# Eight short reads between the sixth and the seventh load of a row-maximum kernel

## The chip, the cores and the metric

The kernel runs on one core of a Trainium2 chip. The metric is device time in microseconds; a time is the median of its runs. A span is that of one profiled execution, between the first and the last instruction that the profiler saw, and is somewhat shorter than the time.

## The reference

```python
def setup_inputs():
    batch, seq, dim = 32, 512, 1024
    return {"x": np.random.randn(batch, seq, dim).astype(np.float32)}

def reference(x):
    return np.max(x, axis=-1).astype(np.float32)
```

The input is 32 x 512 = 16384 rows of 1024 float32, 67.11 MB. Each row gives one number, its maximum; the output is 65.5 KB. Every input element is read once and takes part in one comparison.

## The kernel before

The 16384 rows are seen as 128 partitions with 128 row indices each. A load brings n row indices of all partitions, so 128 x n rows or n x 512 KB, into a ring of 47 places in on-chip memory. The loads' sizes are in BLOCKS: 18 large ones, and then four pieces (PIECES) that bring the last two row indices in parts.

```python
BLOCKS = [
    [2, 15, 16, 14, 11, 11, 10, 10, 8, 8, 7],
    [3, 3, 3, 2, 1, 1, 1],
]
RING = 47
PIECES = [(532, 492), (592, 432)]
```

All loads are issued by SyncE (SP in the profile), one after the other. A load is issued in the program's order as soon as its places in the ring have been read by the work that stands before it:

```python
    def issue():
        nonlocal issued
        while issued < len(loads):
            start, n, src, _ = loads[issued]
            if any(readers[j] and s < start + n and start < s + k
                   for j, (s, k, _, _) in enumerate(loads[:issued])):
                return
            load = nc.sync.dma_start(out=rows(issued), in_=src)
            issued += 1
        ...
        while pieces:
            nc.sync.dma_start(out=pieces[0][0], in_=pieces[0][1])
            pieces.pop(0)
```

VectorE (DVE) does most of the maxima, a load at a time, with one instruction along the last axis:

```python
    def maximum(out, in_):
        return in_turn("DVE", nc.vector.reduce_max(out=out, in_=in_, axis=X))
    ...
    def direct(j):
        _, n, _, col = loads[j]
        m = shared[j][0]
        k = 0 if lead[j] else m
        maximum(res[:, col + k:col + k + n - m], rows(j)[:, k:k + n - m, :])
```

A part of the last loads is shared with the other engines: TensorE (PE) transposes it, ScalarE (ACT) copies it out of PSUM, GpSimd (POOL) reduces over the partitions, and TensorE brings the result back (`turn` and `back` in the whole kernel). The order in which all of it is written down is PLAN: d is a whole reduction on VectorE, t and b the way over the other engines, p, m and f the rest.

The waits are not written in the kernel. The language's scheduling layer works them out and gives every DMA a completion semaphore. It has eight of them for DMAs and hands them out in turn, in the program's order, numbered 0 to 7: the first load has number 0, the eighth number 7, the ninth number 0 again. A DMA that is given a semaphore whose last user may still be under way is made to wait for that user's completion.

Of the kernel before, what the change touches and what calls it, by code (L numbers as in the profile page):

```python
# [8 lines left out]
F32 = mybir.dt.float32  # L9
# [31 lines left out]
def kernel(  # L41
# [5 lines left out]
    nc = tc.nc  # L47
# [10 lines left out]
    once = ctx.enter_context(tc.tile_pool(name="once", bufs=1))  # L58
# [12 lines left out]
    def in_turn(engine, inst):  # L71
        if engine in latest:
            tc.add_manual_dep(inst.ins, latest[engine].ins.name, NOSYNC, reason="in turn")
        latest[engine] = inst
        return inst

    def maximum(out, in_):
        return in_turn("DVE", nc.vector.reduce_max(out=out, in_=in_, axis=X))  # L78

    ident = once.tile([P, P], F32)  # L80
    colno = once.tile([P, P], F32)
    rowno = once.tile([P, 32], F32)
# [3 lines left out]
        out=colno, data0=ident, data1=ident, initial=-1.0, op0=ALU.add, op1=ALU.mult))  # L86
    in_turn("DVE", nc.vector.transpose(out=rowno, in_=colno[:, :32]))  # L87
    for q in range(1, P // 32):
        part = rowno[q * 32:(q + 1) * 32, 0:1]
        in_turn("DVE", nc.vector.tensor_scalar(  # L90
            out=part, in0=part, scalar1=float(q * 32), scalar2=None, op0=ALU.add))
    identity = in_turn("DVE", nc.vector.tensor_scalar(  # L92
        out=ident, in0=colno, scalar1=rowno[:, 0:1], scalar2=None, op0=ALU.is_equal))
# [41 lines left out]
    def rows(j):  # L135
        start, n, _, _ = loads[j]
        return ring[:, I + start * D:I + (start + n) * D].rearrange("p (i d) -> p i d", d=D)
# [90 lines left out]
    issued = 0  # L228
    behind = None
# [7 lines that stand above are left out]
                return  # L237
            load = nc.sync.dma_start(out=rows(issued), in_=src)  # L238
            issued += 1
        if any(readers[j] and s < at + last + 1 and at < s + k for j, (s, k, _, _) in enumerate(loads)):  # L240
            return
        while pieces:
            nc.sync.dma_start(out=pieces[0][0], in_=pieces[0][1])
            pieces.pop(0)

    for step in PLAN:
        issue()
        kind, k = step[0], int(step[1:])
        if kind in "dp":
            (direct if kind == "d" else partial)(k)  # L250
            readers[k] -= 1
        elif kind == "t":
            turn(k)
            readers[chunks[k][0]] -= 1
        elif kind == "b":
            back(k)
        elif kind == "m":
            merge(k)
        else:
            inst = maximum(*tail[k])  # L260
            if behind is None:
                behind = inst
# [34 lines left out]
```

## Time and profile before

| | before |
|---|---|
| time, median of 3 runs | 163.78 us (163.76 to 163.86) |
| span of the profiled execution | 162.1 us |
| busy: DVE | 135.3 us (83%) |
| busy: POOL | 15.9 us (10%) |
| busy: PE | 13.6 us (8%) |
| busy: ACT | 6.3 us (4%) |
| read from HBM | 67.11 MB, 414 GB/s over the span |

The profile's page gives busy time by engine, the same in 40 equal slices (each digit is the busy share of a slice in tenths, 9 for 90% or more), the DMA queues, the chain of work that ended last, the groups of instructions, and the DMA issues with the time from issue to landing. In a line on a wait, such as "A <- B", A is the engine that stood idle, and B what ended its wait; the numbers after it are microseconds in total, the number of waits and the longest of them. Questions put to the trace give the same for a stretch of time. Times in it are counted from the start of the span.

### The profile page before, as it was taken

To read this page: it belongs to the slowest core of one execution; us is meant where nothing else is said; L and a number is where in the kernel's file an instruction comes from. 1 tells how busy PE (TensorE), PEld (TensorE's weight loads), DVE (VectorE), ACT (ScalarE), POOL (GpSimd) and SP (SyncE) were. 2 spreads that over 40 slices of the span, in tenths; PEclk is the share of its full clock that TensorE was granted. 3 is DMA by queue.
4 is the path that set the end of the run, shared out by engine and by line. 5 is a ranking of instruction groups with operands and counts; after the bars stand their busy time and mean duration, and the time that the engine had idled before them with its cause. 6 is when DMAs were issued, how large, how long until landed. Compare 5 with 4: busy or idle time off the path is not lost.

```text
span 162.1 us, 295 instructions
## 1 busy us (share of the span) xinstructions
PE 13.6 (8%) x76; PEld 11.7 (7%) x76; DVE 135.3 (83%) x33; ACT 6.3 (4%) x7; POOL 15.9 (10%) x10
## 2 busy tenths in 40 slices
PE   0000000000000000000000000000000000772942
PEld 0000000000000000000000000000000000762731
DVE  3500019998399999999999999996999999999994
ACT  3000000000000000000000000000000000241120
POOL 0000000000000000000000000000000000099791
PEclk9999999999999999999999999999999999996555
DMA  5995999599879999898999799799999989999991
GB/s 178 566 485 258 470 501 517 259 517 517 354 340 439 453 404 534 356 523 367 478 411 475 334 485 475 334 485 388 477 429 388 466 382 446 415 421 416 411 388 34
DMA packets 3456, 67.18 MB, mean 414 GB/s; under 512 B 640, under 2 KB 896, under 8 KB 1536
## 3 DMA queue, kind: packets, MB, share of 16 engines
q1 hardware_dynamic: 3168, 67.11, 96.8%
q10 hardware_dynamic: 288, 0.07, 0.2%
HBM read 67.11 MB, written 0.07 MB: 414 GB/s over the span
## 4 chain that ended last, share of the span: by engine, by line
DMA 50%; DVE 47%; SPq 1%; issue 0%; DVEq 0%
DMA ring<-in_x_dram 50%; DVE ring L78 45%; DVE joint L78 2%; SPq L238 1%; DVEq L292 0%
## 5 line engine op out<-in xcount | busy, mean ns | idle before, releaser
L78 DVE TENSOR_REDUCE ring<-ring 128x1 f32<-128x1024 f32 (+13 forms) x20 | 129.9, 6547 | 23.5 <-DMA ring<-in_x_dram 23.5
L168 POOL PARTITION_ALL_REDUCE top<-sb x6 | 15.7, 2658 | 142.6 <-ACT sb L166 142.5
L160 PE MATMUL ps<-ident,ring 128*128 128x128 f32 x38 | 9.0, 423 | 140.0 <-DMA ring<-in_x_dram 140.0
L160 PEld LDWEIGHTS ps<-ident,ring 128*128 128x128 f32 x38 | 7.6, 225 | 140.1 <-issue 140.1
L166 ACT COPY sb<-ps 128x1024 f32<-128x1024 f32 (+2 forms) x6 | 5.0, 834 | 150.5 <-PE ps L160 143.5
L78 DVE TENSOR_REDUCE joint<-ring 128x2 f32<-128x1280 f32 (+1 forms) x3 | 3.9, 1314 | 0.0
L178 PE MATMUL got<-ident,top 1*128 1x1 f32 x24 | 2.7, 228 | 3.8 <-POOL top L168 3.6
L178 PEld LDWEIGHTS got<-ident,top 1*128 1x128 f32 x24 | 2.4, 188 | 4.6 <-POOL top L168 4.6
L178 PE MATMUL joint<-ident,top 1*128 1x1 f32 x14 | 2.0, 244 | 1.9 <-POOL top L168 1.9
L178 PEld LDWEIGHTS joint<-ident,top 1*128 1x128 f32 x14 | 1.7, 210 | 2.7 <-POOL top L168 2.7
L166 ACT ACT_TABLE_LOAD x1 | 1.3, 1283 | 0.7 <-PEq L281 0.7
L83 DVE MEMSET ident<- 128x128 f32 x1 | 0.2, 165 | 0.8 <-PEq L281 0.8
L90 DVE TENSOR_SCALAR rowno<-rowno 32x1 f32<-32x1 f32 x3 | 0.4, 146 | 0.1
L85 DVE TENSOR_TENSOR_SCAN colno<-ident 128x128 f32<-128x128 f32 x1 | 0.4, 425 | 0.0
L92 DVE TENSOR_SCALAR ident<-colno,rowno 128x128 f32<-128x128 f32 x1 | 0.3, 288 | 0.0
L87 DVE STREAM_TRANSPOSE rowno<-colno 128x32 f32<-128x32 f32 x1 | 0.2, 211 | 0.0
L78 DVE TENSOR_REDUCE ring<-got 128x3 f32<-128x24 f32 x1 | 0.2, 172 | 0.0
L78 DVE TENSOR_REDUCE ring<-joint 128x5 f32<-128x20 f32 x1 | 0.2, 170 | 0.0
L281 POOL MEMSET const-float32-0.0<- 128x1 f32 x1 | 0.1, 98 | 0.2 <-issue 0.2
L281 POOL MEMSET const-bfloat16-1.0<- 128x1 bf16 x1 | 0.1, 102 | 0.0
L281 POOL MEMSET const-uint8-127<- 128x1 uint8 x1 | 0.1, 101 | 0.0
L281 POOL MEMSET const-float32-1.0<- 128x1 f32 x1 | 0.1, 98 | 0.0
(1 smaller groups left out, 0.1 us busy)
## 6 DMA issues: line engine op xcount, KB each, us to landing
ring<-in_x_dram SPq DMA_DIRECT2D x2, 5632.0 KB, 29.9
ring<-in_x_dram SPq DMA_DIRECT2D x2, 5120.0 KB, 36.8
ring<-in_x_dram SPq DMA_DIRECT2D x2, 4096.0 KB, 32.5
ring<-in_x_dram SPq DMA_DIRECT2D x1, 7680.0 KB, 22.6
ring<-in_x_dram SPq DMA_DIRECT2D x1, 7168.0 KB, 58.0
ring<-in_x_dram SPq DMA_DIRECT2D x3, 1536.0 KB, 35.7
ring<-in_x_dram SPq DMA_DIRECT2D x1, 3584.0 KB, 29.2
ring<-in_x_dram SPq DMA_DIRECT2D x2, 1024.0 KB, 17.8
```

Source lines behind the costliest of these rows:

```text
L78: return in_turn("DVE", nc.vector.reduce_max(out=out, in_=in_, axis=X))
L83: in_turn("DVE", nc.vector.memset(ident, 1.0))
L85: in_turn("DVE", nc.vector.tensor_tensor_scan(out=colno, data0=ident, data1=ident, initial=-1.0, op0=ALU.add, op1=ALU.mult))
L87: in_turn("DVE", nc.vector.transpose(out=rowno, in_=colno[:, :32]))
L90: in_turn("DVE", nc.vector.tensor_scalar(out=part, in0=part, scalar1=float(q * 32), scalar2=None, op0=ALU.add))
L92: identity = in_turn("DVE", nc.vector.tensor_scalar(out=ident, in0=colno, scalar1=rowno[:, 0:1], scalar2=None, op0=ALU.is_equal))
L160: in_turn("PE", nc.tensor.transpose(out=ps[:, w:w + P], in_=rows(j)[:, lead[j] + r + i, c * P:(c + 1) * P], identity=ident,))
L166: in_turn("ACT", nc.scalar.copy(out=sb[:, :W], in_=ps[:, :W]))
L168: in_turn("POOL", nc.gpsimd.partition_all_reduce(top[:, :W], sb[:, :W], P, bass_isa.ReduceOp.max))
L178: in_turn("PE", nc.tensor.transpose(out=share(j)[:, r + i, c:c + 1], in_=tops[k][0:1, w:w + P], identity=ident[0:1, 0:1],))
L238: load = nc.sync.dma_start(out=rows(issued), in_=src)
L281: nc = _bacc.Bacc("TRN2", target_bir_lowering=False, num_devices=1)
```

## The change

After the sixth load is issued, and before the seventh, eight more reads are put on the same queue. Each reads the first few elements of a row of the sixth load's source, in the first 2, 3, 4, 6, 8, 10, 12 and 14 partitions: 16 elements (64 B) a partition in the first, four more in each that follows, 44 elements (176 B) in the last. They go to a small tile of their own, which nothing reads. So the results do not depend on them; the reads put transfers of different widths and packet sizes between two large ones, all of which use 128 partitions, which may change how the sixteen DMA engines stand against each other from there on.

```diff
@@ -77,6 +77,7 @@
     def maximum(out, in_):
         return in_turn("DVE", nc.vector.reduce_max(out=out, in_=in_, axis=X))
 
+    short = once.tile([16, 8 * 64], F32)
     ident = once.tile([P, P], F32)
     colno = once.tile([P, P], F32)
     rowno = once.tile([P, 32], F32)
@@ -237,6 +238,11 @@
                 return
             load = nc.sync.dma_start(out=rows(issued), in_=src)
             issued += 1
+            if issued == 6:
+
+                for q, k in enumerate((2, 3, 4, 6, 8, 10, 12, 14)):
+                    nc.sync.dma_start(out=short[:k, q * 64:q * 64 + 16 + 4 * q],
+                                      in_=src[:k, 0, :16 + 4 * q])
         if any(readers[j] and s < at + last + 1 and at < s + k for j, (s, k, _, _) in enumerate(loads)):
             return
         while pieces:
```

On SyncE the built program has 30 DMA issues instead of 22: the eight stand between the second load of 11 row indices and the first of 10. On the other engines the order of instructions is as before.

## Prediction

> **What bounds the kernel now.** I began with the digits and totals of the page, to see which engine has no idle time where it counts.
>
> ```profile
> DVE  3500019998399999999999999996999999999994
> ...
> DMA  5995999599879999898999799799999989999991
> ...
> q1 hardware_dynamic: 3168, 67.11, 96.8%
> ```
>
> Two rows are nearly full. VectorE (DVE) has holes in the first twelve slices, of 4.05 us each, and hardly any later; the DMA engines carry their one big queue, q1, for 96.8% of the span. Both cannot be the limit, so I looked at three stretches of the body in the view by windows. Its columns after the time are busy microseconds of PE, its weight loads, DVE, ACT and POOL, then the clock, the DMA share and GB/s.
>
> ```profile
> 5.60:43.00 37.40, 0.00 (x0) 0.00 (x0) 18.44 (x2) 0.00 (x0) 0.00 (x0) 1.00 1.00 433
> 43.00:86.70 43.70, 0.00 (x0) 0.00 (x0) 43.57 (x3) 0.00 (x0) 0.00 (x0) 1.00 0.98 426
> 86.70:139.00 52.30, 0.03 (x1) 0.06 (x1) 50.98 (x6) 0.00 (x0) 0.00 (x0) 1.00 0.99 427
> ```
>
> In the first stretch VectorE works 18.44 of 37.40 us while the transfers run at 433 GB/s with a share of 1.00; later VectorE is full too, but the rate stays at 426 and 427. One row index of the input is 128 x 4096 B = 0.524 MB, so at 433 GB/s it takes 1.21 us to arrive; VectorE needs 17.22 us for the 16 rows of the third load, 1.08 us a row. So **the transfers are the bound**, VectorE trails them by little, and a microsecond in which no transfer runs is not won back. The chain that ended last says "DMA 50%; DVE 47%", which I do not read as half and half: the two are so close that it changes from one to the other.
>
> VectorE's waits for data confirm that loads arrive late and not VectorE:
>
> ```profile
> DVE ring L78 <- DMA ring<-in_x_dram: 23.5, 4, 15.8
> ```
>
> The change works in the queue of issues, so I asked when the two loads around it are issued and land. Numbering the loads from the first to the twenty-second, the trace gives one issue at 60.38 us (the sixth, 11 rows) and the next at 60.76 us (the seventh, 10 rows). The view of DMA issues in that window gives KB each and the time from issue to landing:
>
> ```profile
> ring<-in_x_dram SPq DMA_DIRECT2D x1, 5632.0 KB, 26.3
> ring<-in_x_dram SPq DMA_DIRECT2D x1, 5120.0 KB, 38.1
> ```
>
> The sixth lands at 60.38 + 26.3 = 86.7 us, the seventh at 60.76 + 38.1 = 98.8 us. The second landing is 12.1 us after the first, and 5120 KB = 5.243 MB at 433 GB/s is 12.1 us: no gap between them. That is so because the seventh was issued 26 us before the sixth ended. VectorE's reduction of the seventh load begins at 98.8 us, at its landing, so there is no reserve on that side either.
>
> **What the Trainium skill says.** "DMA: Bandwidth & Descriptors", section "Anatomy of one DMA — SWDGE (gpsimd) path", says that DMA engines do not wait on semaphores; the sequencer that issues does, and the engines consume what is queued. The trace agrees: in SyncE's own waits the loads of line 238 wait 90.8 us for VectorE and the transfers run on. The same page, section "Why a DMA increments its semaphore by 16 and not by 1", says that a hardware-queued DMA uses the largest number of engines up to 16 that divides its outermost size, the lowest-numbered ones: so the eight reads would take 2, 3, 4, 6, 8, 10, 12 and 14 of the 16. No trace here shows that yet. The section "Bandwidth" derives 435 GB/s from the ports of the on-chip memory; the 433 GB/s above fits, and leaves nothing to be gained by better order.
>
> **The change part by part.** It removes nothing and adds eight reads on SyncE's queue and 2 KB in 16 partitions.
>
> *Bytes.* 2 x 64 B up to 14 x 176 B sum to 8.3 KB against 67.11 MB: 0.02 us at 433 GB/s. The descriptors are 2+3+4+6+8+10+12+14 = 59. The 448-byte store packets in this trace take about 25 ns each, so even the lowest engine, with eight of them, is busy for some 0.2 us more. Nothing computes on them.
>
> *Issues.* An issue on SyncE takes 327 to 613 ns. Eight are some 3.3 us of SyncE's time, and SyncE has more than that to spare: between 60.8 and 75.4 us it only waits. By duration alone the change is free.
>
> *Waits.* Here I looked at the waits that the built program places on SyncE. Its DMAs take eight completion semaphores in turn, and one that comes round to a semaphore still in use waits for its last user to land. In the kernel before, the seventh load is the first user of the seventh semaphore and is issued with no wait. With the short reads the turn goes: reads one to five take the semaphores numbered 6, 7, 0, 1, 2 and wait for nothing that is not done; read six takes number 3 and waits for the fourth load (issued at 2.1 us and landed 58.0 us later, at about 60 us, so no cost); read seven takes number 4 and waits for the fifth (40.0 + 33.4 = 73.4 us); read eight takes number 5 and **waits for the sixth load, the one just in front of it** (86.7 us). SyncE issues in order, so the seventh load stands behind that wait. When it is issued, nothing is left in the queue: the engines stand dry.
>
> *How long they stand dry.* SyncE wakes at once: the pieces of line 243 are issued some 0.02 us after the landing that they wait for. Issue of the eighth read, with the gap to the next, 0.38 us (the distance of the two issues at 60.38 and 60.76). So the seventh load is issued at 86.7 + 0.02 + 0.38 = 87.1 us. A load into an empty queue is seen once before, the first of the kernel: 1024 KB, 4.9 us from issue to landing. Its bytes are 1.049 MB / 433 GB/s = 2.42 us, so filling an empty queue costs 4.9 - 2.42 = 2.48 us. By that the seventh load lands at 87.1 + 2.48 + 12.1 = 101.7 us against 98.8 us: **2.85 us later**. The first load is a cold one; its first packets begin about 1.0 us after the issue, and take 0.5 to 1.2 us where later ones of the same size take 0.31. The two small stores at the end, into an idle queue of their own, take 1.6 and 1.4 us in all, though they read on-chip memory and not the input. If a restart costs no more than they do, the loss is nearer 1.8 us. A restart reads from the main memory again, so I keep near the first load and choose 2.65 us.
>
> *After it.* The semaphores of the short reads are free by then. The eighth load follows 0.4 us after the seventh, for its place was freed at about 75 us; the ninth too (87.2 us). From there the queue is as deep as before, VectorE starts its part of the seventh load at its landing in both kernels, and the tail hangs on the last landings. I expect a rigid shift of everything by the same amount. The sum: 163.78 + 2.65 = 166.4 us, 1.6% more.
>
> **Rivals.** *Hidden anyway:* the wait costs nothing, and the time stays within 0.2 us of 163.8. For it: 8.3 KB, and SyncE idle. Against it: the wait is for the transfer itself, not for something beside it, and the queue holds nothing else. It needs the seventh load to be queued before 86.7 us, which the order of waits excludes.
>
> *Uneven engines:* the reads go to the low-numbered engines only, each with a packet of another size, and put the sixteen out of step, or break up a step that hurts; 0.2 us on one engine each way. Against a gain: the share is 1.00 at 433 GB/s already. A loss of more than 0.2 us would take short packets that hold up a ring for about a microsecond each, which would add to the dry time and lead to some 168 us. The 4-byte completion packets between loads take 9 ns and the next data packet follows on, which speaks against it.
>
> *VectorE as the bound:* if it had slack to make up, part of 2.65 us would come back; the 0.14 us per row between its rate and the transfers' only lets it catch up with them, never ahead of them. I give it nothing.
>
> **Range and chances.** The low end of the dry time, 1.8 us, gives 165.6; the cold one with a slower issue of the eighth read and some tenths for the short packets, 3.2 us, gives 167.0. I take 165.7 to 167.0. The 2% line is at 163.78 x 1.02 = 167.06 us, 3.3 us away: 0.10 for slower by more than that, 0.02 for faster, and 0.88 for within 2%.
>
> **What would show it.** The profile after should have one dip of the DMA digits and GB/s just past 86.7 us and none elsewhere; the seventh load issued at about 87.1 us, where it was 60.8; from its issue to its landing 14 to 15 us where it was 38.1; in SyncE's waits for DMA, two new ones, of some 10 us for the fifth load and 13 us for the sixth; VectorE idle for a fifth time, by 2.65 us, at about 98.9 us; bytes, counts of work on PE, ACT and POOL and the durations of the reductions unchanged. The prediction is wrong if the DMA share stays full there, if the restart takes under 1.5 or over 3.5 us, or if the landings after the seventh do not all move by the same amount.

## The result and the profile after

| | before | after |
|---|---|---|
| time, median of 4 runs | 163.82 us (163.76 to 163.87) | 166.76 us (166.68 to 166.86) |
| ratio, 95% interval | | 1.018 (1.0162 to 1.0198) |
| span of the profiled execution | 162.1 us | 165.0 us |

The changed kernel is 1.8% slower, by 2.94 us. The page of after, first the rows of digits and the big queue, q1:

```profile
DVE  3500029996599999999999993996999999999994
...
DMA  5999599969999989999888899979989999999991
...
q1 hardware_dynamic: 3286, 67.12, 95.6%
```

VectorE has a new hole, the 3 in its twenty-fifth slice (99 to 103 us). The DMA row has 8s around 87 us, where its lowest digits before the tail, a 5 and a 6, stand in the first nine slices; it doesn't show what happened, and why is seen below. q1 has 3286 - 3168 = 118 more packets. In the trace they are 59 short rows of 64 to 176 B, and 59 more packets of 4 B, the completions. If each read finished on all 16 engines, there would be 128 completions; so a read of k partitions ran on k engines, as the Trainium skill says for these widths ("DMA: Bandwidth & Descriptors", section "Why a DMA increments its semaphore by 16 and not by 1"). That these are the lowest-numbered engines no run here shows.

VectorE's waits for data, and SyncE's own waits (L239 issues the loads, L244 the short reads); the columns are total us, times, longest:

```profile
DVE ring L78 <- DMA ring<-in_x_dram: 26.3, 5, 15.8
```

```profile
SPq L239 <- DVE ring L78: 64.9, 5, 17.2
SPq L239 <- DMA ring<-in_x_dram: 33.5, 4, 21.0
SPq L244 <- DMA ring<-in_x_dram: 23.7, 2, 13.0
```

VectorE waits a fifth time for data, for 26.3 - 23.5 = 2.8 us. SyncE has two waits that belong to the short reads: the longest 13.0 us, the other 10.7 us.

The chain that ended last says the rest, in order of time (start, length, what):

```profile
60.38 26.33 DMA ring<-in_x_dram
86.71 0.02 issue
86.73 0.32 SPq L244
87.04 0.04 issue
87.09 14.58 DMA ring<-in_x_dram
101.67 0.02 issue
101.69 10.83 DVE ring L78
```

The sixth load is issued at 60.38 us and lands at 86.71, as before. SyncE wakes, issues the eighth short read, and then, at 87.09 us, the seventh load, which was issued at 60.76 us before. It lands 14.58 us later, at 101.67 us instead of 98.82. Of the 14.58 us, 12.12 are its bytes at the rate of before; 2.46 us is the price of starting an empty queue.

The view by windows around that point (columns as before, the last two DMA share and GB/s), first of the kernel before and then of the changed one, and the changed one's DMA view of the same stretch, in 40 slices of 0.07 us:

```profile
86.30:89.00 2.70, 0.00 (x0) 0.00 (x0) 2.70 (x2) 0.00 (x0) 0.00 (x0) 1.00 0.84 364
```

```profile
86.30:89.00 2.70, 0.00 (x0) 0.00 (x0) 2.70 (x2) 0.00 (x0) 0.00 (x0) 1.00 0.76 228
```

```profile
DMA  0000000000000000000010000099999900000090
...
DMA packets 43, 0.62 MB, mean 228 GB/s; under 512 B 28, under 2 KB 28, under 8 KB 28
```

The share falls only from 0.84 to 0.76 and the rate from 364 to 228 GB/s, because these views, and the rows of the page, count a packet with all of its time and all of its bytes in the slice in which it starts. (So the share of a short stretch can pass 1: 1.25 in the kernel before from 74 to 76 us.) The 43 - 28 = 15 long packets that start in these 2.7 us start from 88.09 us on, and the first of them ends at 90.26 us, outside. With every packet of the trace cut at the edges of the stretch, the share is 0.26 in the changed kernel and 1.00 in the kernel before. From 86.26 us, where the last long packet of the sixth load ends, to 88.09 us only packets of the short reads and completions run: the engines do stand dry. Of the 2.46 us, 1.0 us passes between the issue and the first packet; the first packet on each engine then takes 1.6 to 2.4 us, where later ones take 1.51.

After that the stream is as before, in the view of the kernel before and of the changed one:

```profile
98.85:139.00 40.15, 0.03 (x1) 0.06 (x1) 38.83 (x5) 0.00 (x0) 0.00 (x0) 1.00 0.99 426
```

```profile
101.70:141.86 40.16, 0.03 (x1) 0.06 (x1) 38.83 (x5) 0.00 (x0) 0.00 (x0) 1.00 0.99 426
```

From the landing of the seventh load to that of the eleventh the rate is 426 GB/s in both, so nothing is lost or won there. The last load lands 2.86 us later than before. The 0.08 us by which the time's 2.94 us exceed that are within the spread of the runs.

### The profile page after: what moved, and what is told of

The parts are those of the page before. It is cut to its first block, busy times and chain, and to the rows that moved or that the text cites. A ratio compares the mean times of both kernels' runs of the same rounds, so it can differ in the third digit from the quotient of the medians.

```text
span 165.0 us, 303 instructions
## 1 busy us (share of the span) xinstructions
PE 12.8 (8%) x76; PEld 11.0 (7%) x76; DVE 135.4 (82%) x33; ACT 6.3 (4%) x7; POOL 15.9 (10%) x10
## 3 DMA queue, kind: packets, MB, share of 16 engines
q1 hardware_dynamic: 3286, 67.12, 95.6%
## 4 chain that ended last, share of the span: by engine, by line
DMA 74%; DVE 23%; SPq 1%; issue 0%; DVEq 0%
DMA ring<-in_x_dram 74%; DVE ring L78 20%; DVE joint L78 2%; SPq L239 1%; SPq L244 0%; DVEq L298 0%
## 5 line engine op out<-in xcount | busy, mean ns | idle before, releaser
L78 DVE TENSOR_REDUCE ring<-ring 128x1 f32<-128x1024 f32 (+13 forms) x20 | 130.0, 6547 | 26.3 <-DMA ring<-in_x_dram 26.3
L161 PE MATMUL ps<-ident,ring 128*128 128x128 f32 x38 | 8.1, 389 | 142.9 <-DMA ring<-in_x_dram 142.9
L161 PEld LDWEIGHTS ps<-ident,ring 128*128 128x128 f32 x38 | 6.7, 206 | 143.0 <-issue 142.9
```

What stands on the lines that cost most here:

```text
L161: in_turn("PE", nc.tensor.transpose(out=ps[:, w:w + P], in_=rows(j)[:, lead[j] + r + i, c * P:(c + 1) * P], identity=ident,))
```

## The experiments

**The same reads on another queue.** ScalarE issues them behind the fourth load; SyncE's loads are held in their order.

```diff
-            load = nc.sync.dma_start(out=rows(issued), in_=src)
+            load = in_turn("SP", nc.sync.dma_start(out=rows(issued), in_=src))
-                    nc.sync.dma_start(out=short[...], in_=src[...])
+                    read = in_turn("ACT", nc.scalar.dma_start(out=short[...], in_=src[...]))
+                    tc.add_manual_dep(read.ins, fourth.ins.name, SYNC, reason="behind the fourth")
```

> The same eight reads of the same widths, but issued by ScalarE instead of SyncE, all behind the landing of the fourth load (about 60 us), and SyncE's loads kept in their order. SyncE then waits for no large load but as before; the loads wait for short reads only. Theory of the wait: the seventh load is queued well before the sixth lands at 86.7 us, no dry time, 163.8 us within 0.3. Rival, the short packets or the uneven use of the engines cost by themselves: the reads are all there, so 166 to 167 us.

Measured: 163.96 us, ratio 1.001 (1.0003 to 1.0017). SyncE's waits between 59 and 90 us:

```profile
SPq L241 <- DMA short<-in_x_dram: 32.2, 3, 26.3
SPq L241 <- DVE ring L78: 13.4, 2, 11.4
```

The only DMAs that SyncE waits for here are short reads, in a stretch in which the queue has large loads in it: in the trace the seventh load is issued at 69.8 us and lands at 98.82 us. (The eighth read takes the semaphore of the fifth load, so ScalarE issues it only at 73.5 us; no load waits for it there.) Widths, packets and unequal engines are all there, and cost 0.13 us by the medians (0.05 to 0.28 by the interval). The rival that the reads cost by themselves falls.

**Six of the eight reads.**

```diff
-                for q, k in enumerate((2, 3, 4, 6, 8, 10, 12, 14)):
+                for q, k in enumerate((2, 3, 4, 6, 8, 10)):
```

> The first six of the eight reads, on SyncE as in the change. The seventh load now takes the semaphore of the fifth load and waits for 73.4 us, the eighth load that of the sixth (86.7 us) with the seventh already queued. Theory of the wait: no dry time, 163.8 us within 0.2. Rival, a cost by read or by packet: six of eight reads or 33 of 59 packets, so 1.6 to 2.2 us of the 2.9, 165.4 to 166.0 us.

Measured: 164.18 us, ratio 1.0024 (1.0015 to 1.0032). That is 0.35 us over before, more than the 0.2 that I allowed, and far under the 1.6 of the rival. SyncE's waits between 60 and 90 us:

```profile
SPq L239 <- DMA ring<-in_x_dram: 23.7, 2, 13.0
SPq L239 <- DVE ring L78: 17.6, 2, 17.2
```

The two waits of 10.7 and 13.0 us are there to the tenth, and hardly cost anything: the seventh load has the first of them and is in the queue when the eighth has the second. The last load lands 0.10 us later in this trace, and from the landing of the last store to the end of the span 0.95 us pass where it was 0.83. The cause of that second part, and whether it makes up the rest of the 0.35 us, is not shown.

**The wait alone, without any short read.** The seventh load is issued behind the landing of the sixth.

```diff
-            load = nc.sync.dma_start(out=rows(issued), in_=src)
+            load = in_turn("SP", nc.sync.dma_start(out=rows(issued), in_=src))
+            if issued in (6,):
+                tc.add_manual_dep(load.ins, ahead.ins.name, SYNC, reason="behind the one ahead")
+            ahead = load
```

> No short read at all: the kernel before, with one wait added, the seventh load is issued only when the sixth has landed (86.7 us). Theory of the wait: issued at 86.72 us, 0.37 us earlier than in the changed kernel, filled and landed at 86.72 + 2.46 + 12.12 = 101.3 us, 2.5 us later than before; 166.3 us. Rival, the short reads cost: 163.8 us.

Measured: 166.20 us, ratio 1.0148 (1.0133 to 1.0163), 2.4 us lost with no short read in the program. From the chain:

```profile
60.26 26.31 DMA ring<-in_x_dram
86.57 0.02 issue
86.58 14.66 DMA ring<-in_x_dram
101.24 0.02 issue
```

The same picture, without the issue of a short read between. 14.66 - 12.12 = 2.54 us of start.

**Eight reads over all partitions**, so that all engines have the same share.

```diff
-    short = once.tile([16, 8 * 64], F32)
+    short = once.tile([P, 8 * 64], F32)
     ...
-                for q, k in enumerate((2, 3, 4, 6, 8, 10, 12, 14)):
-                    nc.sync.dma_start(out=short[:k, ...], in_=src[:k, 0, :16 + 4 * q])
+                for q in range(8):
+                    nc.sync.dma_start(out=short[:, ...], in_=src[:, 0, :16 + 4 * q])
```

> Eight reads of the same row lengths in the same place, but each over all 128 partitions, so that all engines get the same share; 1024 packets instead of 59. The order of waits is that of the change. Theory of the wait: dry time as in the change, the added packets of the first seven reads lie in it; 166.7 us, up to 0.4 more if the packets hold up the rings. Rival, the loss comes from engines put out of step by narrow reads: 163.8 to 164.6 us.

Measured: 166.83 us, ratio 1.0189 (1.0172 to 1.0206): the loss of the change, though 1024 packets take the place of 59 and no engine is preferred. Width and number of packets make no difference to this loss; what wide reads would cost in a full queue is not shown.

**Seven reads**, so that the seventh load itself takes the semaphore of the sixth.

```diff
-                for q, k in enumerate((2, 3, 4, 6, 8, 10, 12, 14)):
+                for q, k in enumerate((2, 3, 4, 6, 8, 10, 12)):
```

> The first seven of the eight reads, one more than the run with six, which took 164.2 us. Now the seventh load itself takes the semaphore of the sixth and is issued at its landing, 86.73 us. Theory of the wait: the loss jumps from 0.3 to about 2.5 us, as with the wait alone, and stays 0.37 us under that of eight: 166.2 to 166.5 us. Rival, a cost by read: the seventh adds as much as each of the six before it, 0.1 us or less, so 164.3 us.

Measured: 166.40 us, ratio 1.0151 (1.0136 to 1.0166). One read of 12 rows of 160 B more than in the run with six, and 2.2 us more. From the chain:

```profile
86.67 0.02 issue
86.69 14.63 DMA ring<-in_x_dram
101.32 0.03 issue
```

It is the loss of the wait alone. A cost that comes all at once with the seventh read is one of the turn of semaphores, not of reads.

**All eight, four on each side of the seventh load.**

```diff
-            if issued == 6:
-                for q, k in enumerate((2, 3, 4, 6, 8, 10, 12, 14)):
+            if issued in (6, 7):
+                for q, k in tuple(enumerate((2, 3, 4, 6, 8, 10, 12, 14)))[4 * (issued - 6):4 * (issued - 5)]:
```

> All eight reads on SyncE's queue, with the widths of the change, but four before the seventh load and four between it and the eighth. The read that waits for the sixth load now has the seventh load queued in front of it. Theory of the wait: no dry time, 163.9 to 164.3 us, as with six reads. Rival, anything that comes from eight such reads on this queue, whatever stands between them: 166.7 us.

Measured: 163.99 us, ratio 1.0007 (0.9998 to 1.0016): no difference that can be told from before. SyncE's waits (L243 issues the short reads here):

```profile
SPq L239 <- DMA ring<-in_x_dram: 31.0, 3, 20.9
SPq L243 <- DMA ring<-in_x_dram: 23.6, 2, 13.0
```

Set beside the changed kernel, this line is the most useful of all. The short reads wait the same 23.7 and 23.6 us for the same two loads, with the same longest wait. One kernel loses 2.9 us and the other 0.1 us; the difference is one load in the queue.

**Sixteen reads**, the eight twice over.

```diff
-                for q, k in enumerate((2, 3, 4, 6, 8, 10, 12, 14)):
+                for q, k in enumerate((2, 3, 4, 6, 8, 10, 12, 14) * 2):
```

> The eight reads twice, sixteen in a row. Reads nine to sixteen take semaphores of short reads that have landed, but stand behind the eighth, which is issued at 86.73 us. Theory of the wait: each further issue of some 0.33 us lengthens the dry time, eight of them by 2.6 us; the seventh load is issued at 89.7 us and lands at about 104.3 us; 163.8 + 2.9 + 2.6 = 169.3 us (168.9 to 169.8). Rival, the reads hide behind a fixed wait once it is there: 166.7 us.

Measured: 169.51 us, ratio 1.0339 (1.0323 to 1.0354). From the chain:

```profile
86.67 0.02 issue
86.69 0.31 SPq L246
...
89.70 0.04 issue
89.74 14.76 DMA ring<-in_x_dram
```

The seventh load is issued at 89.74 us and lands at 104.50 us. Issues on SyncE, which cost next to nothing with a load in the queue (0.13 us for all eight reads in the run before this one), count in full when it holds none: 89.74 - 86.69 = 3.05 us for nine of them.

**Two waits, without any short read**: the wait of the third run on two loads.

```diff
+            if issued in (6, 8):
+                tc.add_manual_dep(load.ins, ahead.ins.name, SYNC, reason="behind the one ahead")
```

> No short read; the seventh load waits for the landing of the sixth, and the ninth for that of the eighth, so the queue runs dry twice. Theory: each restart costs the same, 2.4 us by the run with one such wait, and nothing later makes up for it: 163.8 + 4.8 = 168.6 us (168.3 to 169.0). Rival, VectorE's backlog or the deeper queue behind takes back a part: 167.0 to 168.0 us. A second restart that costs less than the first would speak for a cold part in the first.

Measured: 168.56 us, ratio 1.0287 (1.0271 to 1.0302), 4.7 us lost, twice the 2.4 of one wait. In the trace the ninth load, of 4.194 MB (9.69 us at 433 GB/s), is issued at 113.31 and lands at 125.31 us, so the second start took 12.00 - 9.69 = 2.3 us. There is no cold part that only the first one pays, and VectorE gives nothing back.

## Why the prediction was right

The measured 166.76 us lies in the range of 165.7 to 167.0 us, 0.33 us above 163.78 + 2.65 = 166.43.

*The bound.* Right: where the transfers stop, the time is lost, once (2.4 us), twice (4.7 us) or longer (5.6 us with sixteen reads). It was even clearer than I read it: the 426 and 427 GB/s of the later stretches come from counting packets where they start. With the packets cut at the edges, their bytes spread evenly over their time, all three stretches have 432 to 434 GB/s. (The 0.14 us a row between the two rates should read 0.13; nothing hangs on it.)

*Bytes, packets, widths.* Right: on another queue or on two sides of a load all eight cost 0.13 us by the medians, which is hardly clear of the noise, and widening them to all partitions leaves the loss as it was. Only the run with six reads, at 0.35 us, is above the 0.2 us that I allowed.

*The order of waits.* Right in each of its parts: the waits of 10.7 and 13.0 us, the issue at 87.09 us (87.1 predicted), no dry time with six reads, the jump with seven.

*How long the engines stand dry.* The mechanism was right and one term too small. The step from the kernel's first load gave 2.48 us of start and 2.85 us in all; measured were 2.46 and 101.67 - 98.82 = 2.85 us. I then took 0.2 us off, for a warm restart and with the stores at the end as the lower bound. That discount failed: the starts measured in the changed kernel, with one wait and the second of two waits are 2.46, 2.54 and 2.3 us, about the 2.48 of the first load. (The first packets of the first load take 0.31 to 1.22 us in the trace, not 0.5 to 1.2; no sum rests on it.) The stores, at 1.4 and 1.6 us, were no model for it; which of their differences from a load makes them shorter is not shown. The 0.2 us, 0.09 us between the shift of the landings and that of the time, and 0.04 us by which the time before rose with its fourth run (163.78 to 163.82) together make up the 0.33 us.

*A rigid shift.* Right: +2.85 us at the seventh load, +2.86 us at the last, and 2.84 to 2.88 us at every one between.

*What was to show it.* I had said that the digits would show a dip, and that a full DMA share there would speak against me. The digits showed none, and the share in the window fell only from 0.84 to 0.76: a poor sign, because both count a packet where it starts. The packets themselves show the dip, 0.26 against 1.00.

## What to carry to other kernels

When transfers bound a kernel, judge an inserted one by what its issue waits for and what is then left in the queue, not by its bytes. With a fixed number of completion semaphores handed out in turn, a run of small transfers uses up the turn, and the one that comes round to the load just ahead empties the queue; spread them so that a large load always stands between. A wait of 13 us that leaves a load in the queue cost 0.1 to 0.35 us here, and the same wait that leaves none cost 2.4 us and every issue that follows it. And where a stretch is not much longer than a packet, look at when packets start and end before you trust a share or a rate.

## What the runs showed of the hardware

Restarting the stream in mid-kernel cost about as much as its first start (2.48 us): 2.3 to 2.6 us in every run with a dry queue, of which about 1.0 us passes before the first packet begins. The short reads were nearly free where they overlapped with a running stream (0.13 us for eight), their packets taking 11 to 14 ns each; but their completions, queued behind one large load, came in at steps of 0.17 to 0.18 us for each read.
